# A two-layer decoder trunk: three instead of four gate rows in the first attention step of layer 2, and the last row beside the output projection

## The chip, the cores and the metric

The kernel runs on one core of one Trainium2 chip. A core has a matrix engine (PE; its weight loads are listed as PEld), a vector engine (DVE), a scalar engine (ACT), GpSimd (POOL), and SyncE (SP), whose queue here issues nearly all loads; POOL's queue issues the stores to scratch memory. The metric is device microseconds of one execution, lower is better. The kernel before has a median of 2121.85 us in three runs (2119.22 to 2122.07).

## The reference, cut to what matters

Layer 1 mixes tokens by retention, layer 2 by latent attention (MLA); 512 tokens, width 2048, everything in float32.

```python
for i in range(2):
    mod = c_act @ ada_w[i] + ada_b[i]              # 2048 -> 3 * 2048
    shift, scale, gate = jnp.split(mod, 3, axis=-1)
    h = rmsnorm(x, norm_g[i]) * (1.0 + scale) + shift
    y = retention_branch(h, ...) if i == 0 else mla_branch(h, ...)
    x = x + gate * y
return rmsnorm(x, final_norm_g)

def mla_branch(h, pos, ...):                       # 16 heads, 128 + 64 rotary, values 128
    cq, ckv, k_rope, g = split(h @ w_in)           # 512, 512, 64, 2048
    q = rmsnorm(cq) @ w_uq                         # per head 128 plain + 64 rotary
    k_nope, v = split(rmsnorm(ckv) @ w_ukv)        # per head 128 + 128
    o = causal softmax attention with rope(q), rope(k_rope)
    return (silu(g) * o) @ w_out
```

The change concerns `gate` of layer 2, a vector of 2048 numbers, `c_act @ ada_w[1][:, 4096:] + ada_b[1][4096:]`. It is used only at the very end of the layer, where the output projection is scaled by it and added to x.

## The kernel before, in words

A float32 product is made of three float32r products of high and low parts (`mm3`, L158 to L160), so each operand is first parted: ACT casts the high part, DVE subtracts it from the whole to get the low part. L135/L136 (`split`) and L1937/L1938 (`parted`) are these two halves of one job.

Layer 2's attention takes its 16 heads in 8 pairs. `attention_step(pr)` runs for pr from -1 to 6. A step computes for the next pair, nx = pr + 1, the queries and keys (`uq`, `uk`) and the values (`uv`), each by PE into a PSUM bank, and, if pr >= 0 (`here` is then not empty), the attention of pair pr in between. The first step (pr = -1) has no attention in it, only the products of pair 0. The products take the banks named `acc`, of which there are four, in turn: uq_2 (the rotary parts of both heads), uq_0, uq_1, uk_0, then uk_1 in the bank that uq_2 had, uv_0 in that of uq_0, uv_1 in that of uq_1. Scores, transposed probabilities and head outputs take the four banks named `aux`.

uq_2 is read twice: by `rope_own` (DVE, L1949, product with the cosines into `qr_t`) and by `rope_swap` (ACT, L1944, four copies of 32 rows into `qr_sw`). DVE then multiplies `qr_sw` by the sines, adds, and both engines part the result into `qr`.

The gate of layer 2 is computed beside the attention, by DVE, in 32 pieces n = 0 to 31. One piece is 128 outputs by one half of the 2048 inputs: `gate_load` fetches 512 KB of the transposed matrix into `mod_gate` (L2159; tag `bw`, two buffers) and, at n = 0 and n = 16, the half of c that belongs to it into `c_gate` (L2153; one of 16 buffers tagged `big`); `gate_sum` multiplies the two and accumulates along the row (L2170). Pieces 0 to 15 use the first half of c, 16 to 31 the second; in each half eight pieces are for outputs 0 to 1023 (part 0), eight for 1024 to 2047 (part 1). After piece 23 and after piece 31 the sums of part 0 and of part 1 become `gate_c` (L1187, L1190). `gate_loads` issues loads while fewer than two are pending. Each of the eight steps calls `gate_sum` four times, 32 in all: two before `rope_own`, and two around the values.

After step 6 follows the output projection ("o2"): its rows are read back from scratch (`o_in`, L2400, tag `k4`), parted into `o_h` and `o_l`, and multiplied with the weights `o_w` in two rounds r of eight units u, 24 matmuls per unit; the attention of the last pair runs in hooks between the units. `o2_hooks(i)` is called ahead of unit i (i = 0 to 15). The first columns of `gate_c` are used after round 0, those of part 1 later still.

The order of instructions on an engine comes from a scheduler, bounded by order marks: `queued(f)` puts what f issues behind everything issued so far on ACT, DVE, PE and SP, `behind(E)` behind the last instruction of the engines named. Each engine and each queue then works strictly in its list's order, so an instruction that waits holds up all that stand behind it.

Of the kernel before, what the change touches and what calls it, by code (L numbers as in the profile page):

```python
# [49 lines left out]
def hybrid_trunk_kernel(  # L50
# [44 lines left out]
    def big(name, dt=F32R):  # L95
        return base.tile([P, 2, T], dt, tag="big", bufs=16, name=name)
# [363 lines left out]
    A_, V_, T_, S_ = (getattr(mybir.EngineType, e) for e in ("Activation", "DVE", "PE", "SP"))  # L460

    @contextmanager
    def behind(*engines):

        with ExitStack() as stack:
            for e in engines:
                ins = next((i for i in reversed(nc.cur_bb.bb.instructions) if i.engine == e), None)
                if ins is not None:
                    stack.enter_context(tc.issue_after(ins))
            yield  # L470

    def queued(fn, *args):
        with behind(A_, V_, T_, S_):
            return fn(*args)  # L474
# [256 lines left out]
    for u in range(1, NU):  # L731

        here, there = ("v", "qk") if u % 2 == 0 else ("qk", "v")
# [451 lines left out]
    def use_modulation(i, sect, part, mc):  # L1185
        both = small(f"mod_{i}_{sect}_{part}_s", 8)
        DVE.tensor_add(both, mc[:, 0, :], mc[:, 1, :])  # L1187
        if sect == 2:
            cols = slice(part * 8, part * 8 + 8)
            DVE.tensor_add(gate_c[i][:, cols], both, gate_bias[i][:, cols])  # L1190
        else:
            modulate(i, both if sect == 0 else None, both if sect == 1 else None, part * 8, 8)
# [814 lines left out]
    def units_ahead():  # L2007
        with behind(S_):
            while unit_state[0] < min(unit_state[1] + 3, len(unit_order)):
                unit_load(*unit_order[unit_state[0]])  # L2010
                unit_state[0] += 1

    def next_unit(kind):

        if unit_state[1] == len(unit_order) or unit_order[unit_state[1]][0] != kind:
            return lambda: None
        low = queued(unit_prepare, *unit_order[unit_state[1]])
        unit_state[1] += 1

        def late():  # L2020
            queued(low)
            units_ahead()

        return late
# [120 lines left out]
    gate_n, gate_pending = [0], []  # L2145

    def gate_load():

        n = gate_n[0]
        j, part, b = n // 16, n // 8 % 2, n % 8  # L2150
        if n % 16 == 0:
            half = gate_c_half[j] = big(f"c_gate{j}", F32)
            nc.sync.dma_start(  # L2153
                half.rearrange("p a n -> p (a n)"),
                c_d[0:1, j * 1024 : (j + 1) * 1024].rearrange("o n -> (o n)").partition_broadcast(P),
            )
        aw = l2_tile("bw", 2, f"mod_gate_{part}{b}{j}", (P, 2, T))
        r0 = 2 * D + (8 * part + b) * P
        nc.sync.dma_start(aw, ada_t[1, r0 : r0 + P, j * 1024 : (j + 1) * 1024].rearrange("p (a n) -> p a n", a=2))  # L2159
        gate_n[0] += 1  # L2160
        gate_pending.append((aw, part, j, b, gate_c_half[j]))

    def gate_loads():
        with behind(S_):
            while gate_n[0] < 32 and len(gate_pending) < 2 and not (gate_n[0] % 16 == 0 and gate_pending):
                gate_load()

    def gate_sum():
        aw, part, j, b, c_half = gate_pending.pop(0)
        DVE.scalar_tensor_tensor(  # L2170
            out=aw, in0=aw, scalar=1.0, in1=c_half, op0=ALU.mult, op1=ALU.mult,
            accum_out=gate_sums[part][:, j, b : b + 1],
        )
        if (j, b) == (1, 7):
            use_modulation(1, 2, part, gate_sums[part])
# [8 lines left out]
    def attention_step(pr):  # L2184

        nx = pr + 1
        here = [attend(2 * pr + s) for s in range(2)] if pr >= 0 else ()
        both = heads2[nx] = {}
        units_ahead()
        gate_loads()  # L2190
        if here:
            (sc0, ex0, no0, tr0, sp0, lg0, va0, re0), (sc1, ex1, no1, tr1, sp1, lg1, va1, re1) = here
            queued(lg0)
            queued(lg1)
        low = next_unit("ukv")
        if here:
            for i in range(NT):
                queued(sc0, i)
            for i in range(NT):
                queued(ex0, i)  # L2200
        low()
        if here:
            no0()
        queued(gate_sum)
        queued(uq_products, nx, 2)
        if here:
            for i in range(NT):
                queued(sc1, i)
            for i in range(2):
                queued(ex1, i)  # L2210
        queued(gate_sum)
        if here:
            for i in range(2, NT):
                queued(ex1, i)
        t1 = queued(rope_own, both["uq", 2], f"qr_{nx}")
        low = next_unit("ukv") if here else lambda: None
        if here:
            no1()
        low()
        gate_loads()  # L2220
        for b in range(2):
            queued(uq_products, nx, b)
        sw = queued(rope_swap, both["uq", 2], f"qr_{nx}")
        low = queued(part_pair, nx, "uq", 0)
        queued(rope_turn, t1, sw)
        queued(low)
        low = queued(part_pair, nx, "uq", 1)
        if here:
            queued(tr0)
        queued(low)  # L2230
        lows = [queued(sp0, j) for j in range(3)] if here else []
        both["qr"] = big(f"qr_{nx}")
        queued(rope_highs, t1, both["qr"])
        for low in lows:
            queued(low)
        queued(rope_lows, t1, both["qr"])
        for b in range(2):
            queued(uk_products, nx, b)
            low = queued(part_pair, nx, "uk", b)
            low_w = next_unit("uq")  # L2240
            queued(low)
            low_w()
        if here:
            queued(va0)
            queued(re0)
            queued(tr1)
            for low in [queued(sp1, j) for j in range(3)]:
                queued(low)
        for j in range(2):
            queued(uv_products, nx, j, (1,))  # L2250
        for j in range(2):
            queued(uv_products, nx, j, (0, 2, 3))
            queued(gate_sum)
            gate_loads()
            queued(queued(part_values, nx, j))
        if here:
            queued(va1)
            queued(re1)
# [9 lines left out]
    for pr in range(NPR - 1):  # L2268
        steps.append(Step(multiply=lambda pr=pr: attention_step(pr)))
# [135 lines left out]
    def o2_sums(u):  # L2405

        e, o = (o2_in[u][:, i, :] for i in range(2))
        f0 = tmp(f"o2_s{u}f", (P, 2, H))
        if u < 4:
            f1 = tmp(f"o2_t{u}f", (P, 2, H))  # L2410
        else:
            f1 = late_sums3[u] = l2_tile(*(("sg", 3) if u < 7 else ("rot", 2)), f"o2_t{u}f", (P, 2, H))
        DVE.tensor_add(f0[:, 0, :], e[:, H:], o[:, H:])
        DVE.tensor_sub(f0[:, 1, :], f0[:, 0, :], e[:, :H])
        DVE.tensor_sub(f1[:, 0, :], e[:, :H], e[:, H:])
        DVE.tensor_sub(f1[:, 1, :], o[:, :H], f0[:, 1, :])
        tag, bufs = ("big", 16) if u < 4 else ("k4", 8)
        s = sums3[2 * u] = base.tile([P, 2, 2, H], F32R, tag=tag, bufs=bufs, name=f"o2_s{u}")
        split(f0, s[:, :, 0, :], s[:, :, 1, :])
        if u < 4:  # L2420
            s = sums3[2 * u + 1] = l2_tile("pt", 4, f"o2_t{u}", (P, 2, 2, H), F32R)
            split(f1, s[:, :, 0, :], s[:, :, 1, :])
# [5 lines left out]
    def o2_residual(kt):  # L2428
        tag, bufs = ("sg", 3) if kt >= 13 else ("pp", 5)
        o2_res[kt] = l2p.tile([P, T], F32, tag=tag, bufs=bufs, name=f"o2_xr{kt}")  # L2430
        nc.sync.dma_start(o2_res[kt], x1_d[kt * P : (kt + 1) * P, :])

    def o2_hooks(i):
        l2_hooks.get(i, lambda: None)()
        if 5 < i < 14 and sums3[2 * (i - 6)] is None:
            with behind(V_, A_):
                o2_sums(i - 6)
        if i in (13, 14, 15):
            with behind(S_):
                seven[i - 13].units[0][0]()  # L2440
                if i == 14:
                    for kt in range(4, 8):
                        o2_residual(kt)
        if i == 15:
            with behind(V_, A_):
                seven[0].units[0][1]()
# [333 lines left out]
```

## Time and profile before

| | |
|---|---|
| median of three runs | 2121.85 us |
| the profiled execution's own time | 2121.05 us |
| its span, first to last instruction | 2119.3 us |
| PE busy | 2100.3 us (99%) |
| DVE busy | 1680.8 us (79%) |
| ACT busy | 1054.2 us (50%) |
| mean granted TensorE clock | 0.998 |
| first attention step (pr = -1) | from about 1677 us of the span to 1702.7 |
| last attention step (pr = 6) | to about 1923.7 us |
| first unit of the output projection | from 1926.94 us |

In the rows of the timeline the columns are the start in us of the span, the duration in us, the engine (SPq is SP's DMA queue), the line, the operation, the tiles written and read, sizes, and the number of merged instructions; in brackets, how long the engine stood idle before it and what ended that. A granted clock of 1.00 is full speed of the matrix engine.

### The profile page before, as it was taken

Reading aid. Unit: us, or ns where it says so; the run is one execution under the profiler, and the core shown is the slowest. Engines: PE = TensorE matmul, PEld = TensorE weight load, DVE = VectorE, ACT = ScalarE, POOL = GpSimd, SP = SyncE. Lnnn points to the kernel's source line nnn. Section 1 sums busy time; section 2 is a strip of 40 time slices with the busy share of each in tenths; the row PEclk is TensorE's granted clock in tenths of the full one; section 3 lists DMA queues with packets and bytes.
Section 4 is the critical chain, followed back from the end, with each engine's and each line's share of the span. In section 5 each row is a group of like instructions: output and inputs, shape, how many; then the busy total and the mean of one; then the engine's idle time right before and its main releaser. Section 6 shows DMA issues by size and latency. Waiting matters only on the chain.

```text
span 2119.3 us, 30416 instructions
## 1 busy us (share of the span) xinstructions
PE 2100.3 (99%) x11268; PEld 1815.7 (86%) x11268; DVE 1680.8 (79%) x2562; ACT 1054.2 (50%) x1626; POOL 103.8 (5%) x177
## 2 busy tenths in 40 slices
PE   8999999999999999999999999999999999999998
PEld 6888898989889888888888888898889889898898
DVE  7899888888888789666777778768978688888665
ACT  6764444444454444434344444445446566665343
POOL 1001010000000000000000000010001000000000
PEclk9999999999999999999999999999999999999999
DMA  9975786868777778855657566753456645454453
GB/s 381 407 282 196 249 274 219 286 210 278 230 263 254 243 229 279 266 171 198 222 174 244 194 204 226 260 189 110 162 190 205 199 150 191 145 195 163 147 169 126
DMA packets 237303, 465.08 MB, mean 219 GB/s; under 512 B 21169, under 2 KB 91857, under 8 KB 233569
## 3 DMA queue, kind: packets, MB, share of 16 engines
q1 hardware_dynamic: 224512, 423.17, 60.0%
q0 software_dynamic: 11920, 38.91, 4.7%
q8 instruction: 88, 1.44, 0.3%
q10 hardware_dynamic: 722, 1.06, 0.1%
q14 instruction: 61, 0.50, 0.1%
HBM read 420.06 MB, written 43.00 MB: 219 GB/s over the span
## 4 chain that ended last, share of the span: by engine, by line
PE 92%; DVE 3%; DMA 3%; ACT 1%; issue 1%; SPq 0%; POOL 0%; DVEq 0%; POOLq 0%; ACTq 0%
PE o L1486 14%; PE x L884 2%; PE x L883 2%; PE y L884 2%; PE s L884 2%; PE y L883 2%; PE s L883 2%; PE x L885 2%; PE s L885 2%; PE y L885 2%; PE o L2601 2%; PE uv L2046 2%; PE qk L158 2%; PE s_qk L984 2%; PE x_qk L984 2%; PE qk L160 2%
## 5 line engine op out<-in xcount | busy, mean ns | idle before, releaser
L1486 PE MATMUL o<-o_h,o_p 128*128 128x512 f32 (+1 forms) x1088 | 322.9, 377 | 0.0
L1486 PEld LDWEIGHTS o<-o_h,o_p 128*128 128x128 f32 x1088 | 200.2, 188 | 37.1
L1486 PE MATMUL o<-o_l,o_p 128*128 128x512 f32 (+1 forms) x544 | 204.8, 377 | 0.0
L136 DVE TENSOR_TENSOR o_p<-o_r,o_p 128x1024 fp32r<-128x1024 f32 x64 | 78.1, 1221 | 51.5 <-ACT o_p L135 51.0
L1486 PEld LDWEIGHTS o<-o_l,o_p 128*128 128x128 f32 x544 | 102.3, 188 | 18.2
L1170 DVE SCALAR_TENSOR_TENSOR mod<-mod,c_odd 128x1024 f32<-128x1024 f32 x56 | 67.2, 1219 | 14.6 <-DMA mod<-in_ada_t_dram 14.6
L135 ACT CAST o_p<-o_r 128x1024 fp32r<-128x1024 f32 x64 | 66.7, 1053 | 20.8 <-PE o L1486 7.8
L158 PE MATMUL qk<-hT,qk_p 128*128 128x512 f32 x192 | 75.0, 391 | 0.0
L160 PE MATMUL qk<-hT,qk_p 128*128 128x512 f32 x192 | 74.8, 390 | 0.0
L159 PE MATMUL qk<-hT,qk_p 128*128 128x512 f32 x192 | 74.7, 389 | 0.0
L389 DVE SCALAR_TENSOR_TENSOR aw<-aw,c_all 128x2048 f32<-128x2048 f32 (+1 forms) x37 | 73.2, 1997 | 1.5 <-DMA aw<-in_ada_t_dram 1.4
L1332 ACT ACTIVATE yn<-y,nmr,gn_r 128x512 f32<-128x512 f32 x32 | 22.3, 777 | 67.7 <-DVE nmr L1326 67.7
L158 PE MATMUL o<-o_h,o_w 128*128 128x512 f32 x128 | 50.1, 391 | 0.0
L160 PE MATMUL o<-o_h,o_w 128*128 128x512 f32 x128 | 49.8, 389 | 0.0
L159 PE MATMUL o<-o_l,o_w 128*128 128x512 f32 x128 | 49.8, 389 | 0.0
L1170 DVE SCALAR_TENSOR_TENSOR mod<-mod,c_bm 128x1024 f32<-128x1024 f32 x40 | 48.7, 1218 | 0.0
L448 PE MATMUL g<-hT,g_p 128*128 128x512 f32 x192 | 46.1, 389 | 0.0
L2046 PE MATMUL uv<-ukv_p,kvT 128*128 128x256 f32 x384 | 46.1, 279 | 0.0
L136 DVE TENSOR_TENSOR qk_p<-qk_r,qk_p 128x1024 fp32r<-128x1024 f32 x23 | 27.9, 1223 | 22.4 <-ACT qk_p L135 22.4
L2046 PEld LDWEIGHTS uv<-ukv_p,kvT 128*128 128x128 f32 x384 | 45.0, 189 | 0.1
L2601 PE MATMUL o<-o_h,o_w 128*128 128x256 f32 (+1 forms) x208 | 43.5, 306 | 0.0
L158 PEld LDWEIGHTS qk<-hT,qk_p 128*128 128x128 f32 x192 | 36.0, 188 | 7.8 <-ACT g_st L474 0.4
(1735 smaller groups left out, 6312.0 us busy)
## 6 DMA issues: line engine op xcount, KB each, us to landing
mod<-in_ada_t_dram SPq DMA_DIRECT2D x96, 512.0 KB, 5.8
o_r<-in_ret_w_out_dram SPq DMA_DIRECT2D x64, 512.0 KB, 5.4
aw<-in_ada_t_dram SPq DMA_DIRECT2D x28, 1024.0 KB, 9.7
mod_gate<-in_ada_t_dram SPq DMA_DIRECT2D x32, 512.0 KB, 4.6
qk_r<-in_ret_w_in_dram SPq DMA_DIRECT2D x48, 256.0 KB, 3.3
qk_r<-qk_d SPq DMA_DIRECT2D x32, 256.0 KB, 6.0
v_r<-v_d SPq DMA_DIRECT2D x32, 256.0 KB, 5.9
sg<-g_d SPq DMA_DIRECT2D x32, 256.0 KB, 6.3
```

The lines of the kernel that those rows point to most:

```text
L136: DVE.tensor_sub(lo, src, hi.bitcast(F32))
L158: PE.matmul(o, lhs[0], rhs[0], start=first and not seeded, stop=False, skip_group_check=seeded)
L159: PE.matmul(o, lhs[0], rhs[1], start=False, stop=False, skip_group_check=seeded)
L160: return PE.matmul(o, lhs[1], rhs[0], start=False, stop=last, skip_group_check=seeded)
L883: PE.matmul(banks[b], a[0], w[0], start=first, stop=False, skip_group_check=True)
L884: PE.matmul(banks[b], a[0], w[1], start=False, stop=False, skip_group_check=True)
L885: PE.matmul(banks[b], a[1], w[0], start=False, stop=True, skip_group_check=True)
L984: PE.matmul(o, w[wp][:, i, b * P : (b + 1) * P], a[ap], start=first and i + b + k == 0, stop=k == 2, skip_group_check=True,)
L1170: DVE.scalar_tensor_tensor(out=aw, in0=aw, scalar=1.0, in1=silu_c[j], op0=ALU.mult, op1=ALU.mult, accum_out=row_sums[piece][:, j, b : b + 1],)
L1486: PE.matmul(o, w[i][:, ki, c0 + b * P : c0 + (b + 1) * P], a[j], start=first and i + j == 0, stop=last and i == 1, skip_group_check=True,)
L2046: PE.matmul(ps[:, (t % 2) * 256 : (t % 2 + 1) * 256], a[i], w[k], start=t % 2 + i + k == 0 and kt == 1, stop=kt == 3 and i == 1, skip_grou ...
L2601: PE.matmul(banks3[b][:, cols], last_w[u][i][:, ki, b * P : (b + 1) * P], o2_moving(2 * u + ki, cols)[j], start=u + ki + i + j == 0, stop= ...
```

## The change

Four edits, which together keep the 32 pieces and their order but move where they stand.

In the first step (no `here`) the two `gate_sum` calls ahead of `rope_own` are left out, and one call is put behind `rope_lows`, the last DVE work on the rotary query, with a `gate_loads` behind it in place of the one behind the attention's second normalisation. With the two around the values the first step has three. The seven other steps keep four each: 31 pieces. The 32nd is called in `o2_hooks(5)`, behind the last DVE instruction. And `gate_loads` no longer holds back piece 16 (and with it the second half of c) while a piece is pending, since the number of pieces done at that point is now odd.

```diff
     def gate_loads():
         with behind(S_):
-            while gate_n[0] < 32 and len(gate_pending) < 2 and not (gate_n[0] % 16 == 0 and gate_pending):
+            while gate_n[0] < 32 and len(gate_pending) < 2:
                 gate_load()
...
         if here:
             no0()
-        queued(gate_sum)
+            queued(gate_sum)
         queued(uq_products, nx, 2)
         if here:
             for i in range(NT):
                 queued(sc1, i)
             for i in range(2):
                 queued(ex1, i)
-        queued(gate_sum)
-        if here:
+            queued(gate_sum)
             for i in range(2, NT):
                 queued(ex1, i)
         t1 = queued(rope_own, both["uq", 2], f"qr_{nx}")
...
         low()
-        gate_loads()
+        if here:
+            gate_loads()
...
         queued(rope_lows, t1, both["qr"])
+        if not here:
+            queued(gate_sum)
+            gate_loads()
         for b in range(2):
             queued(uk_products, nx, b)
...
     def o2_hooks(i):
         l2_hooks.get(i, lambda: None)()
+        if i == 5:
+            with behind(V_):
+                gate_sum()
```

On DVE in the first attention step, before (`mod_gate` rows are the pieces 0 and 1, `qr_t` the rotary query, `uqT` and `ukT` the parted queries and keys):

```order
L1938 TENSOR_TENSOR ukv_1_p<-ukv_1_r,ukv_1_p 128x2x256 x2
L2170 SCALAR_TENSOR_TENSOR mod_gate_15075,gate_sums_1426<-mod_gate_15075,c_gate_15073 128x1024
L2170 SCALAR_TENSOR_TENSOR mod_gate_15077,gate_sums_1426<-mod_gate_15077,c_gate_15073 128x1024
L1949 TENSOR_TENSOR qr_t_15101<-uq_2_15087,cos_12566 128x512
L1953 TENSOR_TENSOR qr_sw<-qr_sw,sin_12568 128x512
L1954 TENSOR_TENSOR qr_t_15101<-qr_t_15101,qr_sw 128x512
L1938 TENSOR_TENSOR uqT_0_15138<-uq_0_15107,uqT_0_15138 128x512
L1938 TENSOR_TENSOR uqT_1_15143<-uq_1_15120,uqT_1_15143 128x512
L1965 TENSOR_TENSOR qr_15146<-qr_t_15101,qr_15146 64x512 x2
L1938 TENSOR_TENSOR ukT_0_15164<-uk_0_15151,ukT_0_15164 128x512
```

and with the change:

```order
L1938 TENSOR_TENSOR ukv_1_p<-ukv_1_r,ukv_1_p 128x2x256 x2
L1949 TENSOR_TENSOR qr_t_15099<-uq_2_15086,cos_12566 128x512
L1953 TENSOR_TENSOR qr_sw<-qr_sw,sin_12568 128x512
L1954 TENSOR_TENSOR qr_t_15099<-qr_t_15099,qr_sw 128x512
L1938 TENSOR_TENSOR uqT_0_15132<-uq_0_15101,uqT_0_15132 128x512
L1938 TENSOR_TENSOR uqT_1_15137<-uq_1_15114,uqT_1_15137 128x512
L1965 TENSOR_TENSOR qr_15140<-qr_t_15099,qr_15140 64x512 x2
L2170 SCALAR_TENSOR_TENSOR mod_gate_15075,gate_sums_1426<-mod_gate_15075,c_gate_15073 128x1024
L1938 TENSOR_TENSOR ukT_0_15161<-uk_0_15148,ukT_0_15161 128x512
```

Both pieces are gone from ahead of `qr_t`; piece 0 stands behind the six instructions on the query, piece 1 further down, ahead of the values.

On SP at the end of the last attention step, before (`sg_15` is the gate path of head 15, `o_w` are weights and `o_in` rows of the output projection; the two `mod_gate` rows are the pieces 30 and 31):

```order
L142 DMA o_w_2_raw<-in_mla_w_out_dram 128x2x512
L2159 DMA mod_gate_17546<-in_ada_t_dram 128x1024
L2159 DMA mod_gate_17548<-in_ada_t_dram 128x1024
L2400 DMA o_in_17764<-o_d 128x2x512
L2400 DMA o_in_17903<-o_d 128x2x512
L2400 DMA o_in_17960<-o_d 128x2x512
L142 DMA o_w_3_raw<-in_mla_w_out_dram 128x2x512
L2400 DMA o_in_18033<-o_d 128x2x512
L2122 DMA sg_15_17852<-sg_d 128x512
```

and with the change (the first two `mod_gate` rows are now the pieces 29 and 30; `L2403` is what was `L2400`):

```order
L142 DMA o_w_2_raw<-in_mla_w_out_dram 128x2x512
L2159 DMA mod_gate_17543<-in_ada_t_dram 128x1024
L2159 DMA mod_gate_17545<-in_ada_t_dram 128x1024
L142 DMA o_w_3_raw<-in_mla_w_out_dram 128x2x512
L2122 DMA sg_15_17848<-sg_d 128x512
L2159 DMA mod_gate_17716<-in_ada_t_dram 128x1024
L2403 DMA o_in_17760<-o_d 128x2x512
L2403 DMA o_in_17899<-o_d 128x2x512
L2403 DMA o_in_17956<-o_d 128x2x512
```

Piece 31, whose buffer is that of piece 29, is now loaded behind `sg_15`, and every `o_in` stands behind it.

On DVE in the output projection, with the change (`p_` are the probabilities of head 15, `o_l` low parts of the projection's rows):

```order
L136 TENSOR_TENSOR o_l_18083<-o_in_18080,o_h_18082 128x1024
L2170 SCALAR_TENSOR_TENSOR mod_gate_17716,gate_sums_1427<-mod_gate_17716,c_gate_16317 128x1024
L2095 RECIPROCAL rs_17888<-sm_17856 128x4
L136 TENSOR_TENSOR o_l_18122<-o_in_18119,o_h_18121 128x1024
L2103 TENSOR_SCALAR p__17857<-p__17857,rs_17888 128x128
```

Piece 31 comes between the low parts of two of the projection's rows, ahead of the normalisation of head 15.

## The prediction

> **What bounds the kernel now.** I read the page's shares and chain first, then the waits of PE in layer 2's attention and behind it.
>
> ```profile
> PE 2100.3 (99%) x11268; PEld 1815.7 (86%) x11268; DVE 1680.8 (79%) x2562; ACT 1054.2 (50%) x1626; POOL 103.8 (5%) x177
> PE 92%; DVE 3%; DMA 3%; ACT 1%; issue 1%; SPq 0%; POOL 0%; DVEq 0%; POOLq 0%; ACTq 0%
> ```
>
> PE sets the time; a change that leaves PE's instructions as they are, as this one does, can only alter PE's waits and its clock. From 1675 us to the end PE waits only twice:
>
> ```profile
> PE uk L158 <- ACT qr_sw L1944: 3.9, 1, 3.9
> PE x_sums L2642 <- ACT x_sq L2478: 0.2, 1, 0.2
> ```
>
> The first wait lies in the first attention step, and the timeline there shows its cause:
>
> ```profile
> 1678.04 0.43 SPq L2153 DMA_DIRECT2D c_gate<-c_d  x1
> 1679.63 0.39 PE L160 MATMUL uq<-qT,uq_l 128*128 128x512 f32 x1
> 1680.52 1.29 DVE L1938 TENSOR_TENSOR ukv_p<-ukv_r,ukv_p 128x512 fp32r<-128x512 f32 x2
> ...
> 1685.29 0.39 PE L158 MATMUL uk<-kvT,ukv_p 128*128 128x512 f32 x1
> ...
> 1686.65 1.23 DVE L2170 SCALAR_TENSOR_TENSOR mod_gate<-mod_gate,c_gate 128x1024 f32<-128x1024 f32 x1 [4.83 <-DMA c_gate<-c_d]
> 1687.79 0.39 PE L160 MATMUL uk<-kvT,ukv_p 128*128 128x512 f32 x1
> 1687.80 1.22 DVE L2170 SCALAR_TENSOR_TENSOR mod_gate<-mod_gate,c_gate 128x1024 f32<-128x1024 f32 x1
> 1688.95 0.68 DVE L1949 TENSOR_TENSOR qr_t<-uq,cos 128x512 f32<-128x512 f32 x1
> 1689.67 2.34 ACT L1944 COPY qr_sw<-uq 32x512 f32<-32x512 f32 x4 [8.65 <-DVE qr_t L1949]
> 1692.03 1.07 ACT L1937 CAST uqT<-uq 128x512 fp32r<-128x512 f32 x2
> 1692.04 0.69 DVE L1953 TENSOR_TENSOR qr_sw<-qr_sw,sin 128x512 f32<-128x512 f32 x1 [2.40 <-ACT qr_sw L1944]
> 1692.06 0.80 PE L158 MATMUL uk<-kvT,ukv_p 128*128 128x512 f32 x1 [3.88 <-ACT qr_sw L1944]
> ...
> 1697.21 5.70 PE L2046 MATMUL uv<-ukv_p,kvT 128*128 128x256 f32 x48
> ```
>
> uk_1 needs the bank of uq_2, complete near 1680.0 (1679.63 + 0.39). But DVE stands at piece 0 until the half of c lands, does two pieces, and only then `qr_t`; ACT's four copies follow it, and PE with them. And PE does not come back at its old speed:
>
> ```profile
> 1685.00:1688.00 3.00, 3.00 (x15) 2.29 (x13) 1.35 (x3) 0.00 (x0) 0.00 (x0) 1.00 0.71 277
> 1688.00:1692.00 4.00, 0.17 (x1) 0.00 (x0) 1.63 (x3) 2.30 (x4) 0.00 (x0) 0.78 0.54 193
> 1692.00:1697.00 5.00, 4.94 (x12) 3.88 (x13) 4.83 (x8) 3.83 (x8) 0.00 (x0) 0.50 0.16 56
> 1697.00:1703.00 6.00, 6.00 (x53) 5.95 (x52) 4.99 (x9) 2.05 (x5) 0.00 (x0) 1.00 0.60 184
> ```
>
> The third figure from the end is the granted clock: it falls during the wait, is half through uk_1's twelve matmuls, and full again for uv.
>
> **The change part by part.** *The two pieces ahead of `qr_t` go.* uk_0's twelve matmuls start from 1685.29 to 1687.79, a pitch of 2.50 / 11 = 0.227 us. At this pitch uk_1 would start at 1688.02 and uv at 1688.02 + 12 x 0.227 = 1690.74. They started at 1692.06 and 1697.21. So the wait cost 4.04 us, the half clock (1697.21 - 1692.06) - 2.73 = 2.42 us, together **6.47 us**.
>
> Is all of it recovered? With the change DVE takes `qr_t` after `ukv_p`, at 1681.81, to 1682.5; ACT copies to 1684.85 (2.34); the bank is wanted at 1688.02, 3.2 us later. What follows, by the same durations: sines and sum (2 x 0.69) to 1686.2, low parts of uqT (1.28) to 1687.5, which frees the banks that uv takes from 1690.74; the parts of `qr` to about 1688.9. No load still on its way stands on this path any more.
>
> *Piece 0 behind `rope_lows`.* At 1688.9 its data are there (1686.65), so it takes 1.23 us, to 1690.1. Behind it on DVE wait the low parts of ukT and of the next weights, wanted by the scores at 1690.74 + 5.70 = 1696.4. They are six short instructions, 2 x (0.69 + 1.02) = 3.4 us, ready by about 1693.5:
>
> ```profile
> 1696.12 0.69 DVE L1938 TENSOR_TENSOR ukT<-uk,ukT 128x512 fp32r<-128x512 f32 x1
> 1696.73 1.02 DVE L1938 TENSOR_TENSOR uq_l<-uq_r,uq_h 128x256 fp32r<-128x256 f32 x2
> ```
>
> So piece 0 costs nothing there; the cover is uv's 5.70 us, of which about 2.9 are left. Without it, it would cost its 1.23. The loads of pieces 2 and 3 now follow one DVE piece each, and steps 0 to 6 keep their four places; I price them at nothing: PE waits in none of these steps.
>
> *The half of c at piece 16* stays between two `mod_gate` loads in the same step, now one piece further from its use: nothing.
>
> *Piece 31 and its load.* This is the part that can cost. Here is the end of the last step and the start of the output projection before:
>
> ```profile
> 1904.88 1.72 SPq L2400 DMA_DIRECT2D o_in<-o_d  x3
> 1916.09 0.33 SPq L2122 DMA_DIRECT2D sg<-sg_d  x1
> 1917.99 1.22 DVE L2170 SCALAR_TENSOR_TENSOR mod_gate<-mod_gate,c_gate 128x1024 f32<-128x1024 f32 x1
> 1922.63 1.05 ACT L135 CAST o_h<-o_in 128x1024 fp32r<-128x1024 f32 x1
> 1924.50 1.22 DVE L136 TENSOR_TENSOR o_l<-o_in,o_h 128x1024 fp32r<-128x1024 f32 x1
> 1926.94 0.39 PE L158 MATMUL o<-o_h,o_w 128*128 128x512 f32 x1
> 1927.17 0.39 PE L159 MATMUL o<-o_l,o_w 128*128 128x512 f32 x1
> ```
>
> All times here are those of the trace before; PE, DVE and the queue reach this place earlier by the same gain. The load of piece 31 waits for piece 29, now the one at 1917.99, so until 1919.2; `o_in` was issued at 1904.88 and now queues behind that load, at about 1919.65 (0.34 for the issue ahead of it). Its time to landing, over all eight loads and, from the view of the DMAs, for the four issued together at 1904.88, and below them the longest landing, of c's half in the chain of waits:
>
> ```profile
> DMA to landing us min/median/max: 3.6/4.2/5.4
> o_in<-o_d SPq DMA_DIRECT2D x4, 512.0 KB, 4.6
> 1678.04 8.59 DMA c_gate<-c_d
> ```
>
> With the 4.6 of four in a row (the nearest row: a load directly ahead of it) it lands at 1924.25; ACT's part is done at 1925.3, DVE's at 1926.55, and PE wants them at 1926.94 and 1927.17. That is 0.6 us of room: **0** is my value. With 5.4, the longest of `o_in`, PE waits 0.2 us; with 8.59, the longest landing read anywhere in this layer's attention, 3.4 us. The lower end is nothing: PE had no wait there to lose. The next rows, issued 0.4 to 0.5 us apart (1.72 for three), have more time: unit 1 cannot begin before 24 x 0.227 = 5.4 us of unit 0 are done.
>
> Piece 31 itself adds 1.22 us to DVE just ahead of head 15's normalisation:
>
> ```profile
> 1935.00:1940.00 5.00, 5.00 (x24) 4.11 (x23) 5.00 (x16) 2.83 (x9) 0.00 (x0) 1.00 0.43 129
> 1939.39 1.27 DVE L2103 TENSOR_SCALAR p__17861<-p__17861,rs 128x128 f32<-128x128 f32 x4
> 1949.46 1.28 PE L2113 MATMUL pT<-ident,p__17861 128*128 128x128 f32 x10
> 1957.35 1.23 DVE L136 TENSOR_TENSOR o_w<-o_w_raw,o_w 128x1024 fp32r<-128x1024 f32 x1 [4.25 <-ACT o_w L135]
> 1976.74 1.40 DVE L2471 SCALAR_TENSOR_TENSOR x<-o,gate_c,o_xr 128x512 f32<-128x512 f32 x2
> ```
>
> DVE is full there, but PE transposes these probabilities 8.8 us after they were ready (1949.46 against 1940.66), and by 1957 DVE idles 4.25 us: an `o_l` that comes 0.8 us later (1925.3 against 1924.50) and the piece, together some 2.0 us, are absorbed. `gate_c` is used first at 1976.74. Price 0; without that room, 1.2.
>
> Sum: -6.47 + 0 = -6.5 on the span, 2112.8 us; on the execution's own time 2121.05 - 6.5 = **2114.6 us**. The median of the three runs lies 0.8 us above that execution, inside their spread.
>
> [...]
>
> **The rivals.** *A: the output projection gives part back.* `o_in` lands 2 to 4 us late and PE waits there. For it: the move from 1904.88 to 1919.65 uses up nearly all the room. Against: 4.6 us fits. The 8.59 landing gives -6.47 + 3.4 = -3.1, or 2118.0; if the clock falls as in the first step, 2.4 more, 2120.4. [...]
>
> *B: the stall stays in the first step in another place,* since ACT's copies or piece 0 meet something unseen. It needs 3.2 us of lateness for uk_1, or 2.9 for the scores. For it: c's half took 8.59 us to land, the longest row here; but to reach the scores it would have to take some 13.7 (piece 0 from 1688.9 + 2.9, against the issue at 1678.04). Then only the two pieces ahead of `qr_t`, 2.4 us, come off the path: 2121.05 - 2.4 = 2118.6.
>
> *C: slower.* One mechanism: the `o_in` queue behind piece 31. Each microsecond of landing after about 1924.9 is one of PE's wait; with 2.4 for the clock it cancels the gain from a wait of 4.0 us and makes the kernel slower by over 0.2% (4.2 us) from 8.3 us, a landing 13.5 us after its issue. At 14 us it gives 2121.05 - 6.5 + 8.8 + 2.4 = 2125.8. No row near it is longer than 8.59.
>
> **How the numbers follow.** Forecast 0.78, A 0.12, B 0.06, C 0.04. What a measurement of this kernel can tell from no change is about 0.2%, 4.2 us. The forecast and the mild end of A (a wait under 2.2 us) are faster by more: 0.81; the rest of A and B are within: 0.15; C 0.04. The range reaches below the forecast by the spread of the runs (2.0 us under 2114.6), and above to the 2118.0 of A and a little of B: 2112.6 to 2118.6.
>
> **What would show it.** Right: no wait of PE on `qr_sw` from 1675 us on; uk_1 starting 0.23 us after uk_0's last matmul; a granted clock of 1.00 in each stretch of this step; uv from about 1690.7; the whole span near 2112.8. The first piece would start near 1688.9 without a wait for a DMA. The first `o_in` should be issued near 1913.2 in the new span (1919.65 less 6.47), with PE's first matmul on `o_l` not waiting. Wrong: a PE wait on `o_h` or `o_l` at the first unit (A, C), or on anything of ACT or DVE in the first step (B); a median above 2118.6 would mean the room at the output projection was misjudged.

## The result and the profile after

The changed kernel takes 2114.72 us (median of 10 runs, 2113.98 to 2115.78) against 2121.56 us for the kernel before (10 runs beside it, 2118.96 to 2122.23). The ratio is 0.997, with a 95% interval of 0.9961 to 0.998, so 4 to 8 us are gained. The prediction was 2114.6 us.

The profiled execution has 2114.73 us of its own, a span of 2113.0 us and a mean granted clock of 0.999. First its busy shares and the engines' shares of the chain, then what PE waits for from 1670 us on:

```profile
PE 2098.4 (99%) x11268; PEld 1814.2 (86%) x11268; DVE 1680.8 (80%) x2562; ACT 1054.1 (50%) x1626; POOL 103.8 (5%) x177
PE 95%; DMA 3%; DVE 1%; ACT 0%; SPq 0%; issue 0%; POOLq 0%; DVEq 0%
```

```profile
PE o L159 <- DVE o_l L136: 0.3, 1, 0.3
PE x_sums L2648 <- ACT x_sq L2484: 0.2, 1, 0.2
```

The work is the same to the instruction. The wait of 3.9 us on `qr_sw` is gone, and a wait of 0.3 us on `o_l` is new. The timeline of the first attention step:

```profile
1681.23 0.68 DVE L1949 TENSOR_TENSOR qr_t<-uq,cos 128x512 f32<-128x512 f32 x1
1681.95 2.35 ACT L1944 COPY qr_sw<-uq 32x512 f32<-32x512 f32 x4 [1.44 <-DVE qr_t L1949]
1684.79 0.39 PE L158 MATMUL uk<-kvT,ukv_p 128*128 128x512 f32 x1
1687.51 0.39 PE L158 MATMUL uk<-kvT,ukv_p 128*128 128x512 f32 x1
1688.41 1.23 DVE L2170 SCALAR_TENSOR_TENSOR mod_gate<-mod_gate,c_gate 128x1024 f32<-128x1024 f32 x1
1690.23 5.70 PE L2046 MATMUL uv<-ukv_p,kvT 128*128 128x256 f32 x48
```

and the stretches of time there (the third figure from the end is the granted clock):

```profile
1685.00:1688.00 3.00, 3.00 (x15) 2.47 (x14) 2.90 (x6) 2.11 (x4) 0.00 (x0) 1.00 0.69 269
1688.00:1692.00 4.00, 4.00 (x26) 3.61 (x25) 3.97 (x8) 2.64 (x6) 0.00 (x0) 1.00 0.29 100
1692.00:1697.00 5.00, 5.00 (x46) 5.00 (x45) 4.11 (x8) 1.62 (x4) 0.00 (x0) 1.00 0.87 269
```

In this execution uk_0 (the first keys' product, in the rows the first `uk`) starts 0.50 us earlier than in the one before (1684.79 against 1685.29). That is no effect of the change: in experiments 7 to 9, whose first step is that of the changed kernel, it starts at 1685.67, 1685.46 and 1685.37. From there uk_1 follows after 2.72 us, twelve matmuls at full pace, and uv after 5.44 us. Before it took 11.92 us to uv (1697.21 - 1685.29). The first step gains 11.92 - 5.44 = 6.48 us.

A little of it is given back at the output projection:

```profile
1912.27 0.33 SPq L2159 DMA_DIRECT2D mod_gate<-in_ada_t_dram  x1
1912.77 2.93 SPq L2403 DMA_DIRECT2D o_in<-o_d  x5
1918.34 1.05 ACT L135 CAST o_h<-o_in 128x1024 fp32r<-128x1024 f32 x1 [2.69 <-DMA o_in<-o_d]
1919.42 1.23 DVE L136 TENSOR_TENSOR o_l<-o_in,o_h 128x1024 fp32r<-128x1024 f32 x1 [1.80 <-ACT o_h L135]
1919.98 0.40 PE L158 MATMUL o<-o_h,o_w 128*128 128x512 f32 x1
1920.70 0.50 PE L159 MATMUL o<-o_l,o_w 128*128 128x512 f32 x1 [0.32 <-DVE o_l L136]
```

ACT waits for the `o_in` that was queued behind piece 31's load, DVE for ACT, and PE's second matmul comes 0.72 us after its first instead of 0.23 us: 0.49 us are lost. Counted from uk_0 to the end of the span, which leaves the earlier start out, the kernel before takes 434.01 us (2119.3 - 1685.29) and the changed one 428.21 (2113.0 - 1684.79). These 5.80 us of gain are the 6.48 less the 0.49, and less another 0.19 that no row here places.

### The profile page after: what moved, and what is told of

Same layout as the page of the kernel before. It is cut to its first block, busy times and chain, and to the rows that moved or that the text cites. A ratio compares the mean times of both kernels' runs of the same rounds, so it can differ in the third digit from the quotient of the medians.

```text
span 2113.0 us, 30423 instructions
## 1 busy us (share of the span) xinstructions
PE 2098.4 (99%) x11268; PEld 1814.2 (86%) x11268; DVE 1680.8 (80%) x2562; ACT 1054.1 (50%) x1626; POOL 103.8 (5%) x177
## 4 chain that ended last, share of the span: by engine, by line
PE 95%; DMA 3%; DVE 1%; ACT 0%; SPq 0%; issue 0%; POOLq 0%; DVEq 0%
PE o L1486 16%; PE x L884 2%; PE x L883 2%; PE y L884 2%; PE y L883 2%; PE s L884 2%; PE s L883 2%; PE x L885 2%; PE s L885 2%; PE y L885 2%; PE o L2607 2%; PE qk L158 2%; PE s_qk L984 2%; PE x_qk L984 2%; PE qk L160 2%; PE qk L159 2%
```

## The experiments

**1. Are three pieces instead of four needed?** The changed kernel, but both pieces that stood ahead of `rope_own` stand behind `rope_lows`: four in the first step as before, none beside the output projection.

```diff
         if not here:
             queued(gate_sum)
+            queued(gate_sum)
             gate_loads()
...
-        if i == 5:
-            with behind(V_):
-                gate_sum()
```

(The condition on piece 16 in `gate_loads` is that of the kernel before.)

> Pieces 0 and 1 both stand behind the rotary query in the first step; the first step keeps four pieces, nothing is moved to the output projection. Theory of the record (the loss is PE's wait on the bank of uq_2, because the rotary query stands behind pieces that wait for c's half): the whole 6.5 us come off, and the 0.5 us that the changed kernel lost at the first unit of the output projection (PE's wait on o_l) do not arise: span about 2112.4, median about 2114.2, no PE wait in layer 2 from 1675 us to the final sums. Rival (three pieces in place of four is what helps, since the fourth crowds DVE ahead of the scores): PE waits on ukT or the first scores for up to 1.2 us, median 2115.5 or more.

Measured: 2115.13 us (2114.69 to 2115.3, 6 runs), ratio 0.997 (0.9959 to 0.9982). PE's waits from 1670 us on:

```profile
PE x_sums L2646 <- ACT x_sq L2482: 0.2, 1, 0.2
```

The median lies nearer to the rival's 2115.5 than to the theory's 2114.2, but PE has none of the rival's waits. From uk_0 (1685.69) to the end of its span of 2113.2 us this execution takes 427.51 us, 6.50 less than before, where 6.47 were forecast for the first step. So the gain is all here without the fourth piece being moved to the end, and the wait on `o_l` is gone with the load that caused it. What gains is the place behind the rotary query; the number three does nothing that can be measured.

**2. One piece ahead, one behind.** The kernel before, with piece 0 left ahead of `rope_own` and the other behind `rope_lows`.

```diff
-        queued(gate_sum)
         if here:
+            queued(gate_sum)
...
         queued(rope_lows, t1, both["qr"])
+        if not here:
+            queued(gate_sum)
+            gate_loads()
```

> Piece 0 stays ahead of the rotary query, piece 1 goes behind it; four pieces in the first step. The rotary query then starts 1.2 us earlier than before, PE's wait for the bank is about 2.8 us in place of 4.0. Theory (wait and clock are two terms, and a wait this short spares the clock): only the 2.8 us are lost, gain 3.6 us, median about 2118.0, granted clock 1.00 behind the wait. Rival (the clock falls behind any wait of a few us): 2.4 us more are lost, gain 1.2 us, median about 2120.4, granted clock 0.5 for some 5 us.

Measured: 2119.36 us (2117.89 to 2121.47, 10 runs), ratio 0.9991 (0.9982 to 1.0). Timeline and stretches of the first step:

```profile
1686.21 1.23 DVE L2170 SCALAR_TENSOR_TENSOR mod_gate<-mod_gate,c_gate 128x1024 f32<-128x1024 f32 x1 [4.93 <-DMA c_gate<-c_d]
1690.48 0.50 PE L158 MATMUL uk<-kvT,ukv_p 128*128 128x512 f32 x1 [2.84 <-ACT qr_sw L1944]
1692.02 0.63 PE L158 MATMUL uk<-kvT,ukv_p 128*128 128x512 f32 x1
1693.30 0.63 PE L158 MATMUL uk<-kvT,ukv_p 128*128 128x512 f32 x1
1694.58 6.02 PE L2046 MATMUL uv<-ukv_p,kvT 128*128 128x256 f32 x48
```

```profile
1688.00:1692.00 4.00, 1.52 (x6) 1.24 (x7) 1.56 (x4) 3.47 (x7) 0.00 (x0) 0.99 0.37 131
1692.00:1697.00 5.00, 5.00 (x25) 4.40 (x24) 4.91 (x9) 4.07 (x8) 0.00 (x0) 0.67 0.11 10
```

One piece less ahead takes 1.04 us off PE's wait (3.88 to 2.84), about the 1.2 us of the piece; DVE still stands 4.93 us for c's half. The clock reads 1.00 when the wait ends and 1.43 us later falls to 0.50: three matmuls take 1.28 us from 1692.02, at full pace 0.68. From uk_1 to uv pass 4.10 us instead of 2.73, and uv, whose start still falls into the half clock, takes 6.02 us instead of 5.70: the clock costs 1.37 + 0.32 = 1.69 us here. uk_1 starts 3.00 us later than at full pace (1690.48 against 1684.76 + 2.72). Together that is 4.7 us, and by as much this execution takes longer than that of experiment 1 from uk_0 to the end of its span (432.24 us against 427.51). The medians differ by 4.2 us (2119.36 - 2115.13). The result lies between what the two accounts expected: the wait shortens by the piece, and the clock's share shrinks but stays.

**3. Three pieces ahead.** The kernel before with one more instruction like a piece between the two, its product going to a buffer that nothing reads.

```diff
         queued(gate_sum)
+        if not here:
+            queued(gate_again)
         queued(uq_products, nx, 2)
```

> The kernel before with one more piece of the same size on DVE between piece 0 and piece 1, ahead of the rotary query (its product goes to a buffer that nobody reads). Theory: the query, the copies and uk_1 come 1.22 us later, PE's wait is 5.2 us in place of 4.0, the half clock behind it as long as before: 1.2 us slower, median 2122.8 where before has 2121.6. Rival (DVE's place is not what uk_1 waits for): no change, 2121.6.

Measured: 2122.52 us (2121.15 to 2124.04, 10 runs), ratio 1.0005 (0.9995 to 1.0015). Waits and timeline:

```profile
PE uk L158 <- ACT qr_sw L1944: 5.7, 1, 5.7
```

```profile
1687.30 1.23 DVE L2170 SCALAR_TENSOR_TENSOR mod_gate<-mod_gate,c_gate 128x1024 f32<-128x1024 f32 x1 [5.39 <-DMA c_gate<-c_d]
1688.45 1.22 DVE L2179 SCALAR_TENSOR_TENSOR gate_again<-mod_gate,c_gate 128x1024 f32<-128x1024 f32 x1
```

PE's wait grows by 1.8 us: 1.2 for the instruction, the rest from c's half, which landed 0.65 us later in this execution (1687.30 against 1686.65). So here the order on DVE reached PE's wait one to one. The medians settle nothing: this one is 0.8 us above the 2121.7 beside it, and the interval, from -1.1 to +3.2 us, holds no change as well as the 1.8. In the traces, from uk_0 to the end of the span, this execution takes 436.12 us and that of the kernel before 434.01.

**4. Only the other half of the change.** The kernel before, both pieces still ahead, but with three in the first step by leaving out the first of the two around the values; the last piece in `o2_hooks(5)` as in the change.

```diff
             queued(uv_products, nx, j, (0, 2, 3))
-            queued(gate_sum)
+            if here or j == 1:
+                queued(gate_sum)
...
+        if i == 5:
+            with behind(V_):
+                gate_sum()
```

(The condition in `gate_loads` is that of the changed kernel.)

> Only the other part of the change: both pieces stay ahead of the rotary query, one of the two pieces around the values is left out of the first step, and the last piece stands beside the output projection, its load ahead of the projection's rows. Theory: the wait in the first step stays as it was (4.0 us and 2.4 for the clock), and the first unit of the projection waits 0.3 to 0.6 us for o_l: median 2122.1 where before has 2121.6. Rival (one piece less in the first step is worth its 1.2 us): 2120.4.

Measured: 2121.24 us (2119.84 to 2123.32, 10 runs) beside 2121.33, ratio 1.0001 (0.9992 to 1.001). PE's first wait and the clock:

```profile
PE uk L158 <- ACT qr_sw L1944: 3.9, 1, 3.9
```

```profile
1688.00:1692.00 4.00, 0.66 (x2) 0.57 (x3) 1.59 (x4) 3.00 (x6) 0.00 (x0) 0.86 0.64 220
1692.00:1697.00 5.00, 5.00 (x25) 4.28 (x24) 4.87 (x10) 4.38 (x9) 0.00 (x0) 0.77 0.08 34
```

The wait is as long as before, but from uk_1 to uv pass 4.23 us, so the half clock behind it cost 1.50 us here instead of 2.42. Moving the last piece alone is worth nothing, and costs nothing that the medians can tell; in the trace the second matmul of the output projection comes 0.46 us after the first instead of 0.23.

**5. Is it the wait for c's half or the pieces' own 2.4 us? A first try that failed.** The kernel before with c's half for the pieces 0 and 1 loaded earlier into a tile of its own, `c_early`, beside one of the layer's earlier products; c's half for the other pieces is then loaded with piece 2.

```diff
+    def load_early_c():
+        early_c.append(l2_tile("pt", 4, "c_early", (P, 2, T)))
+        nc.sync.dma_start(
+            early_c[0].rearrange("p a n -> p (a n)"),
+            c_d[0:1, :1024].rearrange("o n -> (o n)").partition_broadcast(P),
+        )
+
+    g23[-3].beside["load"].append(load_early_c)
```

> The kernel before, with both pieces ahead of the rotary query as they were, but the half of c for these two pieces is loaded some 14 us earlier into a buffer of its own (one load of 512 KB more in all); the other pieces use c's half as before, loaded after it. Theory (what makes the loss is that the pieces wait for c's half): the two pieces run as soon as DVE and their own loads are there, from about 1681.8 to 1684.6, the copies end near 1687.6, just ahead of uk_1's turn at 1688.0: gain 6.0 to 6.5 us, median about 2115.3. Rival (it is the two pieces' 2.4 us on DVE ahead of the query, wherever the data are): gain at most 4 us, median 2117.5 or more.

Measured: 2123.5 us (2121.8 to 2124.55, 10 runs), ratio 1.0011 (1.0002 to 1.0021). PE's waits and the timeline:

```profile
PE uk L158 <- ACT qr_sw L1944: 3.1, 1, 3.1
PE uq L158 <- ACT sgs L1909: 2.3, 1, 2.3
```

```profile
1672.23 0.34 SPq L2167 DMA_DIRECT2D c_early<-c_d  x1
1679.58 3.44 SPq L1974 DMA_DIRECT2D uq_r<-in_mla_w_uq_dram  x2
1683.06 0.93 SPq L2159 DMA_DIRECT2D mod_gate<-in_ada_t_dram  x2
1688.47 1.23 DVE L2181 SCALAR_TENSOR_TENSOR mod_gate<-mod_gate,c_early 128x1024 f32<-128x1024 f32 x1 [1.45 <-DMA mod_gate<-in_ada_t_dram]
```

The early load itself stood in SP's queue for 10.2 us before it could go out at 1672.23, and held up all that stands behind it, the weights of the queries and the pieces' own rows among them: the `mod_gate` loads went out at 1683.06 in place of 1675.75. That made a wait of 2.3 us in the step's query products and put `mod_gate` in the place of c. It says nothing on the question.

**6. The same question without a load being moved.** The kernel before, with the rows of pieces 0 and 1 multiplied by themselves. It leaves out c's half for these two pieces, so its gate is not the reference's.

```diff
-        gate_pending.append((aw, part, j, b, gate_c_half[j]))
+        gate_pending.append((aw, part, j, b, aw if n < 2 else gate_c_half[j]))
```

> The kernel before with its two pieces still ahead of qr_t, but pieces 0 and 1 multiply their row by itself in place of c's half, which is loaded as before (so the first two of the 32 gate pieces are not the reference's): DVE has the same two instructions of 1.2 us and no wait for c's half. Theory (what stalls is the wait for the landing of c's half, and the pieces' own time fits): the pieces run from about 1681.8 to 1684.3, qr_t to 1685.0, ACT's copies to 1687.4, and uk_1's bank is free before it is wanted at 1688.0: no PE wait in the first step, clock 1.00, about 2115.1 us. Rival (two DVE instructions ahead of the copies already are too many, whatever they wait for): the first step keeps a PE wait of 2 to 3 us on qr_sw, 2118 or more.

Measured: 2115.73 us (2114.91 to 2116.18, 8 runs), ratio 0.9973 (0.9962 to 0.9984). The timeline:

```profile
1681.16 1.23 DVE L2170 SCALAR_TENSOR_TENSOR mod_gate<-mod_gate 128x1024 f32<-128x1024 f32 x1
1683.74 1.23 DVE L2170 SCALAR_TENSOR_TENSOR mod_gate<-mod_gate 128x1024 f32<-128x1024 f32 x1 [1.34 <-DMA mod_gate<-in_ada_t_dram]
1685.61 2.34 ACT L1944 COPY qr_sw<-uq 32x512 f32<-32x512 f32 x4 [5.28 <-DVE qr_t L1949]
1688.00 0.50 PE L158 MATMUL uk<-kvT,ukv_p 128*128 128x512 f32 x1 [0.52 <-ACT qr_sw L1944]
```

The two instructions stand where they stood and PE's wait is 0.52 us in place of 3.88, with a clock of 1.00 behind it; the 0.52 come from the second piece, which met its own load 1.34 us late. So 3.4 of the 3.88 us, and the clock's loss with them, belong to the landing of c's half. Without that 1.34 us the copies would have ended ahead of uk_1's turn, so the pieces' own time fits there. From uk_0 to the end of the span this execution takes 428.49 us, 5.5 less than before. This removes the rival by which two instructions there are too many whatever they wait for.

**7. Is the new wait on `o_l` that of the queue?** The changed kernel, with piece 31's load issued behind the first rows of the output projection; in SP's queue it then stands behind five `o_in`.

```diff
-            while gate_n[0] < 32 and len(gate_pending) < 2:
+            while gate_n[0] < 31 and len(gate_pending) < 2:
...
     queued(o2_parts, 0)
...
+    with behind(S_):
+        gate_load()
```

> The changed kernel, with the load of the last piece issued behind the first rows of the output projection in place of ahead of them. Theory (PE's wait on o_l at the first unit comes from the projection's rows queueing behind that load): the rows are issued some 14 us earlier, the wait goes, 0.5 us of the span come off: span about 2112.5, median about 2114.2. Rival (it comes from the order of ACT and DVE at this place): the wait stays, 2114.7.

Measured: 2114.76 us (2113.77 to 2116.08, 7 runs), ratio 0.9968 (0.9956 to 0.9979). The timeline at the output projection:

```profile
1898.78 1.72 SPq L2403 DMA_DIRECT2D o_in<-o_d  x3
1913.14 0.34 SPq L2159 DMA_DIRECT2D mod_gate<-in_ada_t_dram  x1
1916.53 1.05 ACT L135 CAST o_h<-o_in 128x1024 fp32r<-128x1024 f32 x1
```

The first three `o_in` go out at 1898.78, 14 us sooner; ACT takes the first rows at 1916.53, behind other work of its own and without a wait for a load, and nothing of PE waits on `o_l` any more. From uk_0 (1685.67) to the end of its span of 2113.2 us this execution takes 427.53 us, 6.48 less than before and 0.68 less than the changed kernel. So the cause of the wait is shown. Its price, 0.5 us by the rows and 0.7 by the two spans, is too small for the medians to tell.

**8. A later `o_in`, a miss.** The changed kernel, with the two pending pieces swapped in the last step, so that piece 31's buffer should come free one piece later.

```diff
             queued(uv_products, nx, j, (0, 2, 3))
+            if pr == NPR - 2 and j == 0:
+                gate_pending.reverse()
             queued(gate_sum)
```

> The changed kernel, with the last two pieces of the last step summed in swapped order, so that the buffer for the last piece's load comes free one piece later and the output projection's rows are issued some 3.2 us later still. Theory (past the room, each us of landing is a us of PE's wait): PE waits about 3.5 us at the first unit, 3.2 us slower than the changed kernel, median about 2117.9; if the clock falls behind this wait as in the first step, 2.4 us more, about 2120.3. Rival (the rows' landing is covered by other work of PE): about 2114.7.

Measured: 2114.91 us (2114.39 to 2115.67, 7 runs), ratio 0.9969 (0.9957 to 0.998).

```profile
1913.43 2.74 SPq L2405 DMA_DIRECT2D o_in<-o_d  x5
1918.72 1.05 ACT L135 CAST o_h<-o_in 128x1024 fp32r<-128x1024 f32 x1 [2.41 <-DMA o_in<-o_d]
```

The load took the buffer of whichever piece was summed first, so `o_in` left at 1913.43, 0.66 us later than in the changed kernel's trace and not a piece later. By as much this execution was behind already at uk_0 (1685.46 against 1684.79), so nothing was delayed. It gives no price for lateness.

**9. The price of a late `o_in`.** The changed kernel, with the first `o_in` tile loaded twice, first with other rows.

```diff
         o2_in[u] = k4(f"o2_in{u}", F32)
+        if u == 0:
+            nc.sync.dma_start(o2_in[u], x1_d[: 2 * P, :].rearrange("(k p) n -> p k n", p=P))
```

> The changed kernel, but the first o_in tile of the output projection is loaded twice, first with rows of x1 and then with its own rows, so that its data land one whole load (about 5 us by the changed kernel's own row, 1912.77 to 1918.3) later, and all o_in behind it too. If each further microsecond of landing is one of PE's wait (rivals A and C of the prediction): PE waits about 5 us on o_h or o_l at the first unit and the clock falls for some 5 us behind it, 2114.7 + 5 = 2119.7 without and 2122 with the clock's 2.4. If other work covers it (the attention's last products standing between): 2114.7 and no PE wait above 0.5 us.

Measured: 2120.5 us (2119.36 to 2122.21, 10 runs), ratio 0.9996 (0.9987 to 1.0005) to the kernel before, and 5.8 us above the changed one. The timeline:

```profile
1923.45 1.04 ACT L135 CAST o_h<-o_in 128x1024 fp32r<-128x1024 f32 x1 [0.92 <-DMA o_in<-o_d]
1924.55 1.31 PE L158 MATMUL o<-o_h,o_w 128*128 128x512 f32 x4 [3.83 <-ACT o_h L135]
1928.94 0.40 PE L158 MATMUL o<-o_h,o_w 128*128 128x512 f32 x1
```

The second load of the tile stands 4.0 us in SP's queue until the first has landed. The rows of the first unit land at 1923.45, 5.1 us later than in the changed kernel (1918.34); 0.58 us of that is this execution's later start (uk_0 at 1685.37), so they are 4.5 us late. PE waits 3.83 us. The eleven matmuls from 1924.55 to 1928.94 take 4.39 us instead of 11 x 0.229 = 2.52, another 1.87 us of half clock and of waiting for `o_l`. Less the 0.49 us that the changed kernel loses here itself, that is 5.2 us; from uk_0 to the end of the span this execution takes 433.33 us, 5.1 more than the changed kernel. So nothing covers a late `o_in` past the room already used: about 1.1 us are lost for each, clock included. By the medians that took back nearly the whole gain. One thing moved beside the load: the order of the twelve matmuls and of ACT's casts around it changed a little with the wait.

## Why the prediction was right, point by point

**What bounds the kernel.** Right. Between the two kernels only PE's waits and its clock differ, and experiment 6 shows which load was behind the wait: c's half.

**The sum in the first step.** 6.47 us were forecast, 6.48 are read from uk_0 to uv. uk_1 follows uk_0 at the matmuls' pitch, the clock is 1.00 in each stretch, piece 0 starts at 1688.41, which is the forecast 1688.9 less the 0.50 us by which this execution was ahead, without waiting for a load, and uv at 1690.23 in place of 1690.7 for the same reason. Experiment 1, which gives the same gain with the four pieces kept, and experiment 4, which gives none without the move, put the whole of it there. Rival B, 2118.6 us, fell with that: nothing waits behind the query.

**The output projection.** Here one term was mis-sized, and one of the prediction's own signs of being wrong, a wait of PE on `o_l` at the first unit, is there. The prediction took 4.6 us for the landing of `o_in` behind piece 31's load, found 0.6 us of room, and set the price at 0. The rows show 5.5 us (1912.77 to 1918.3), just past the 5.4 that it had named as the longest and priced at 0.2 us, and 0.49 us were lost. Why it was longer is seen load by load (last figure: us to landing). First the first `o_in` of the kernel before, then, with the change, piece 31's load, the first `o_in` behind it, and the stretch in which they land (last two figures: the DMAs' share and GB/s):

```profile
o_in<-o_d SPq DMA_DIRECT2D x1, 512.0 KB, 3.6
```

```profile
mod_gate<-in_ada_t_dram SPq DMA_DIRECT2D x1, 512.0 KB, 4.6
o_in<-o_d SPq DMA_DIRECT2D x1, 512.0 KB, 5.5
1915.00:1920.00 5.00, 5.00 (x34) 4.63 (x32) 2.43 (x5) 2.25 (x3) 0.54 (x1) 1.00 1.01 360
```

Before, the first `o_in` of its group landed in 3.6 us, the second in 4.6, the third in 5.4. The 4.6 was thus the time of a load behind one that lands in 3.6. Piece 31's load took 4.6 us itself, to 1916.87 (the median of all 32 `mod_gate` loads before was 4.6 too), and the first `o_in` landed 1.4 us behind it; 512 KB at the 360 GB/s of this stretch are 1.46 us. In experiments 4, 8 and 9 piece 31's load took 4.4 to 4.6 us and the one behind it 5.3 to 5.5 as well. The `o_in` behind the first landed later themselves (6.3 us for the second, 9.0 for the fifth), but nothing shows that they held up the first: the group before was as dense, four `o_in` and one `o_w` from 1904.88 to 1907.63.

The effect is rival A's mechanism in its mild form, a wait under 2.2 us, which had been counted within the faster cases. That count, and the 2118.0 us of rival A that the range takes in (a wait of 3.4 us), take a clock that stays full behind such a wait. No run shows that: the clock stayed at 1.00 behind the waits of 0.32 us here and 0.52 us in experiment 6, and fell to 0.50 in or behind each of seven waits of 2.34 to 5.72 us (the table below). Experiment 7 confirms the cause, and experiment 9 that the lateness would have been paid in full, as rivals A and C assumed. What kept C from happening is that `o_in` landed 5.5 us after its issue and not 13.5.

**Piece 31.** Right. It runs at 1932.36 and head 15's normalisation follows at 1934.70:

```profile
1932.36 1.22 DVE L2170 SCALAR_TENSOR_TENSOR mod_gate<-mod_gate,c_gate 128x1024 f32<-128x1024 f32 x1
1934.70 1.27 DVE L2103 TENSOR_SCALAR p__17857<-p__17857,rs 128x128 f32<-128x128 f32 x4
1943.12 1.28 PE L2113 MATMUL pT<-ident,p__17857 128*128 128x128 f32 x10
```

PE transposes the probabilities 7.1 us after they are ready (1943.12 against 1935.97), 8.8 before: 1.7 us of room were used, near the 2.0 forecast, and no wait appeared.

**The time.** The median is 0.1 us from the forecast, closer than the method deserves: the kernel before scatters over several microseconds, and the medians differ by 6.8 us where the spans differ by 6.3. That the profiled execution comes to 2114.73 us is in part luck: the 0.50 us by which it was ahead of the step make up for the 0.49 lost at the output projection. The clock's term of 2.42 us was read from one execution. In experiment 4 it was 1.50 behind the same wait, in experiment 2 it was 1.69 after a wait 1 us shorter, so that term carries an uncertainty of about a microsecond that the working did not name. The prediction read the half clock's cost from uk_1's 5.15 us (1697.21 - 1692.06); in that trace the half clock lasted 6.83 us, of which 1.86 fell into the wait (the table below).

## What to carry to other kernels

In this kernel an instruction that waited for a load held up all that its engine had behind it: DVE stood 4.83 us for c's half, with the rotary query behind it. Before shortening work ahead of a critical hand-over, ask whether that work waits. Two instructions of 1.2 us fitted there (experiment 6); the load that the first waited for made 5.5 of the 6.5 us, through another engine and the matrix clock. When a transfer is queued behind another, take the landing of that one first, from a row of its own kind, and add what one more transfer needs: here 4.6 us from the first one's issue and 1.4 us more, where a group's median of 4.6 us had been taken for the second alone.

## What the runs showed of the hardware

In these traces the granted clock did not follow PE's wait directly: in the kernel before it fell 2.02 us after the wait began, in experiment 2 it fell 1.43 us after the wait had ended. Its changes can be read from the view of stretches, taken in steps of 0.1 us; it reads 1.00 before and after them and 0.50 between. These are the steps of experiment 2 in which it falls and comes back; a mean of 0.57 is read as 1.00 for 0.01 us and 0.50 for the rest:

```profile
1691.90:1692.00 0.10, 0.10 (x2) 0.04 (x1) 0.10 (x1) 0.09 (x1) 0.00 (x0) 0.57 0.00 0
1695.30:1695.40 0.10, 0.10 (x3) 0.10 (x2) 0.10 (x1) 0.10 (x2) 0.00 (x0) 0.86 0.00 0
```

| run | PE waits from, to | half clock from, to | its length | PE's busy time in it |
|---|---|---|---|---|
| before | 1688.18, 1692.06 | 1690.20, 1697.03 | 6.83 | 4.97 |
| experiment 2 | 1687.64, 1690.48 | 1691.91, 1695.33 | 3.41 | 3.41 |
| experiment 3 | 1688.26, 1693.98 | 1692.74, 1699.57 | 6.83 | 5.59 |
| experiment 4 | 1687.45, 1691.34 | 1690.89, 1694.31 | 3.41 | 2.97 |
| experiment 5, first wait | 1680.02, 1682.36 | 1682.28, 1685.70 | 3.41 | 3.34 |
| experiment 5, second wait | 1692.36, 1695.46 | 1695.94, 1699.35 | 3.41 | 3.41 |
| experiment 9 | 1920.72, 1924.55 | 1925.48, 1928.89 | 3.41 | 3.41 |

(All in us.) The half clock lasted 3.41 us in five of the seven cases and 6.83 us in two. Half of PE's busy time in it is an estimate of its cost: 2.48, 1.71 and 1.48 us for the kernel before and experiments 2 and 4, where the rows gave 2.42, 1.69 and 1.50. Why the same wait of 3.9 us cost 2.42 us in one trace and 1.50 in another is not shown, nor how short a wait must be for the clock to stay full: behind 0.52 us (experiment 6) it did, in the wait of 2.34 us (experiment 5) it fell.

The runs with a wait of 2.34 us or more also scattered more. Ten runs each spread over 3.3 us for the kernel before and over 3.6, 2.9, 3.5, 2.8 and 2.9 us in experiments 2, 3, 4, 5 and 9; without such a wait ten runs of the changed kernel spread over 1.8 us, and six to eight runs of experiments 1, 6, 7 and 8 over 0.6, 1.3, 2.3 and 1.3. What makes this scatter was not tested.
